# A hybrid decoder trunk on one core: TensorE's instructions kept in the program's order

## The chip, the core and the metric

The kernel runs on one core of a Trainium2 chip. The core has a matrix engine (TensorE, PE in the profile, with its weight loads shown apart as PEld), three engines for the rest (VectorE or DVE, ScalarE or ACT, GpSimd or POOL) and a queue that issues most of its transfers (SyncE or SP). Each engine works through a list of instructions of its own and waits on semaphores for the others. The metric is the device time of one launch in microseconds (us); less is better. Three runs of the kernel before gave a median of 1935.17 us, from 1935.16 to 1936.64.

## What is computed

Two layers work on 528 tokens (16 meta tokens and 512 of the sequence) of 1024 channels in float32:

```python
for layer in range(2):
    g = norm_gains[layer]
    h = h + 0.5 * rmsnorm(swiglu(rmsnorm(h, g[0]), w_ffn_in[layer, 0], w_ffn_out[layer, 0]), g[1])
    hn = rmsnorm(h, g[2])
    mix = gla_mixer(hn, ...) if layer == 0 else swa_mixer(hn, ..., k_sh, v_sh, ...)
    h = h + rmsnorm(mix, g[3])
    h = h + 0.5 * rmsnorm(swiglu(rmsnorm(h, g[4]), w_ffn_in[layer, 1], w_ffn_out[layer, 1]), g[5])
    if layer == 0:
        k_sh, v_sh = shared_kv(h, kv_norm, w_kv, cos, sin)
```

So there are four feed-forward blocks (FFNs) of 2816 hidden channels. The mixer of layer 0 is chunked gated linear attention with 4 heads; that of layer 1 is attention of 16 query heads in a window of 128 tokens, over keys and values made once. The output drops the meta tokens.

## The kernel before, in words

Channels lie on the 128 partitions and tokens along the free dimension, so a vector of 1024 channels is 8 tiles. Layer 0 works on two groups of tokens, 272 and 256 wide; layer 1 on two of 256, or on all 512 at once where that can be done. Each float32 operand is split into an upper and a lower part (`w` and its rest, made by ScalarE at L226 or L245 and VectorE at L227 or L246), and each product is three matmuls: upper by upper, lower by upper, upper by lower (`mm3s`). All matmuls are issued at L162 (`mm`), transposes at L174.

An FFN runs in four chunks of hidden tiles (`FF_CHUNKS`: 4, 6, 6 and 6 tiles). The first chunk is computed plainly, and `out_proj` then multiplies its hidden tiles by the output weights into banks named `y`. The other three use Strassen's scheme (class `Strassen`): for a hidden tile `head` makes one product, `body` four, `tail` two, each of 12 matmuls. They accumulate in the PSUM banks `a`, `c` and `d`, and between two products ScalarE or VectorE takes an interim value out of a bank. For tile after tile the order is body(current), head(next), tail(current); for the last tile of a chunk there is no next head, and its tail uses a bank of its own, `e`:

```python
def body(self, t):
    self.product(t.c, t, "s1", "t1", True)
    act.activation(t.v, t.c, AF.Copy)                    # L749
    self.product(t.a, t, "s2", "t2", False)
    act.activation(t.u2, t.a, AF.Copy)                   # L751
    self.product(self.d, t, "12", "21", False)
    act.activation(t.g1, self.d, AF.Silu)
    self.product(t.a, t, "s3", "t3", False)
    dve.tensor_tensor(t.v, t.a, t.v, op=ALU.add)         # L755
...
    self.product(c, t, "s4", "22", last)                 # in tail; c is the bank e for the last tile
```

In the profile `a<-zl0f_t,w_s` is the product s2 or s3 of layer 0 (`zl1f_t` of layer 1), `d<-zl0f,w` the product 12, `e<-zl0f,w_s` the product s4 of a last tile, and `a<-zl0f_t,w` the product 22. There are 4 x 3 = 12 ends of such chunks.

A norm needs the sum of squares over all channels: ScalarE squares (L399 and L402), GpSimd adds (L403), short matmuls `st_` with a vector of ones sum over the partitions, VectorE or GpSimd works out the inverse root and a diagonal matrix `dg` (L361 to L383), and a matmul `r_` spreads it over the partitions. In layer 1's attention `sc` are the scores, `ptm` and `pt` transposes of the probabilities, `o` their products with the values; ScalarE and VectorE copy scores out at L1116 and L1117, VectorE scales at L1135 and masks at L1156 and L1157.

Two things set the order of the work. The first is the program itself: pieces of work are Python generators, and `Flow` resumes them by a clock of its own. Every call of `mm` and `transpose` moves that clock on (columns / 2400 us for split operands, else columns / 600 but at least 0.12), `flow.pump()` resumes what is due, and a generator that yields 3.0 goes on 3 us later by that clock. So chains of small steps, such as a norm's, are woven between the matmuls of a large product in the order in which the program issues its instructions. The second is the scheduler of the framework, which runs when the `TileContext` closes: it goes through the program with its own estimates of durations, and gives each engine the list of its instructions in the order in which they become ready, earlier ones in the program first. Where the next matmul of the program isn't ready by these estimates, a later one that is ready goes ahead of it. Semaphores are placed after that.

`kernel` builds the inputs' layout, opens the `TileContext`, calls `trunk_kernel`, which issues everything, and launches.

## Time and profile before

| | |
|---|---|
| median of three runs | 1935.17 us |
| profiled execution | 1931.38 us |
| its span, first to last instruction | 1929.5 us |
| mean granted clock of TensorE | 0.996 |
| DVE busy | 1420.1 us |
| ACT busy | 1001.7 us |
| POOL busy | 215.1 us |
| bytes moved | 174.61 MB, 90 GB/s |

By stages of the span (PE busy us out of the stretch, then DVE and ACT busy us):

| stretch, us | what it is | PE | DVE | ACT |
|---|---|---|---|---|
| 0 to 45 | start, first FFN's first tiles | 36.84 of 45 | 30.88 | 24.81 |
| 45 to 370 | first FFN | 323.21 of 325 | 245.05 | 170.68 |
| 395 to 590 | linear attention | 192.06 of 195 | 117.28 | 77.74 |
| 690 to 1000 | second FFN | 307.27 of 310 | 233.30 | 165.59 |
| 1085 to 1385 | third FFN | 298.95 of 300 | 228.59 | 160.75 |
| 1428 to 1532 | windowed attention | 96.28 of 104 | 90.48 | 61.96 |
| 1600 to 1929.5 | fourth FFN and the end | 316.55 of 329.5 | 241.17 | 165.19 |

A row of the timeline gives the start and the duration in us, the engine, the line of the kernel, the operation, the tiles written and read (buffer numbers left out) with their shapes, the number of instructions merged into the row, and in brackets how long the engine stood idle before it and on whom it waited. A row of waits gives the total, how often, and the longest, in us. A row of the chain of work gives start, duration, engine, tile and line. The duration of a merged row of matmuls includes the run-out of the last one, so two such rows can overlap by some 0.15 us.

### The profile page before, as it was taken

Reading aid. Unit: us, or ns where it says so; the run is one execution under the profiler, and the core shown is the slowest. Engines: PE = TensorE matmul, PEld = TensorE weight load, DVE = VectorE, ACT = ScalarE, POOL = GpSimd, SP = SyncE. Lnnn points to the kernel's source line nnn. Section 1 sums busy time; section 2 is a strip of 40 time slices with the busy share of each in tenths; the row PEclk is TensorE's granted clock in tenths of the full one; section 3 lists DMA queues with packets and bytes.
Section 4 is the critical chain, followed back from the end, with each engine's and each line's share of the span. In section 5 each row is a group of like instructions: output and inputs, shape, how many; then the busy total and the mean of one; then the engine's idle time right before and its main releaser. Section 6 shows DMA issues by size and latency. Waiting matters only on the chain.

```text
span 1929.5 us, 37402 instructions
## 1 busy us (share of the span) xinstructions
PE 1888.9 (98%) x14522; PEld 1798.1 (93%) x14522; DVE 1420.1 (74%) x2868; ACT 1001.7 (52%) x2268; POOL 215.1 (11%) x417
## 2 busy tenths in 40 slices
PE   8999999999999999999999999999998999999997
PEld 7999999999999999999999898989976898989897
DVE  7885858676464788585887786868788779858584
ACT  5663636653245555353574453535645665636363
POOL 2000000321111400000033000000352140000002
PEclk9999999999999999999999999999999999999998
DMA  4332333322113123323351123233421212333331
GB/s 163 104 100 88 103 96 106 114 74 69 45 52 113 56 72 95 102 91 102 99 176 45 61 88 115 87 112 99 132 66 34 77 45 72 98 105 107 101 112 44
DMA packets 102144, 174.61 MB, mean 90 GB/s; under 512 B 11472, under 2 KB 24272, under 8 KB 101968
## 3 DMA queue, kind: packets, MB, share of 16 engines
q1 hardware_dynamic: 101680, 172.11, 28.2%
q8 instruction: 113, 1.85, 0.4%
q14 instruction: 63, 0.52, 0.1%
q10 hardware_dynamic: 288, 0.13, 0.0%
HBM read 170.10 MB, written 2.10 MB: 89 GB/s over the span
## 4 chain that ended last, share of the span: by engine, by line
PE 70%; DVE 19%; ACT 6%; issue 3%; POOL 1%; DMA 0%; SPq 0%; DVEq 0%; ACTq 0%; POOLq 0%
PE y L162 30%; PE x L162 16%; PE a L162 11%; DVE raw L251 5%; PE c L162 4%; DVE w_s L246 3%; DVE w L246 3%; ACT w_s L245 3%; PE d L162 2%; DVE w L227 2%; PE o L162 1%; ACT w L226 1%; PE po L162 1%; DVE hidl0f L775 1%; PE sc L162 0%
## 5 line engine op out<-in xcount | busy, mean ns | idle before, releaser
L246 DVE TENSOR_TENSOR w_s<-raw,w_s 128x512 fp32r<-128x512 f32 x288 | 194.0, 690 | 129.7 <-ACT w_s L245 127.6
L227 DVE TENSOR_TENSOR w<-raw,w 128x512 fp32r<-128x512 f32 x378 | 244.9, 673 | 31.1 <-ACT w L226 29.3
L162 PE MATMUL y<-hidl0f,w 128*128 128x256 f32 (+1 forms) x2112 | 261.0, 285 | 0.0
L162 PEld LDWEIGHTS y<-hidl0f,w 128*128 128x128 f32 x2112 | 258.8, 188 | 0.7
L245 ACT ACTIVATE w_s<-raw 128x512 fp32r<-128x512 f32 x288 | 175.3, 628 | 149.5 <-DVE raw L251 146.0
L162 PE MATMUL y<-hidl1f,w 128*128 128x512 f32 (+1 forms) x1344 | 249.8, 346 | 0.0
L162 PEld LDWEIGHTS y<-hidl1f,w 128*128 128x128 f32 x1344 | 212.0, 188 | 33.9 <-ACT hidl1f L774 0.4
L226 ACT ACTIVATE w<-raw 128x512 fp32r<-128x512 f32 x378 | 209.0, 586 | 46.0 <-PE y L162 39.4
L403 POOL TENSOR_TENSOR acc_post<-acc_post,sq_post 128x256 f32<-128x256 f32 (+1 forms) x72 | 56.9, 791 | 1386.5 <-ACT sq_post L402 1386.0
L251 DVE TENSOR_TENSOR raw<-raw,raw 128x512 f32<-128x512 f32 x288 | 198.0, 687 | 5.5
L246 DVE TENSOR_TENSOR w<-raw,w 128x512 fp32r<-128x512 f32 x216 | 148.3, 687 | 41.5 <-ACT w L245 40.2
L245 ACT ACTIVATE w<-raw 128x512 fp32r<-128x512 f32 x216 | 133.9, 621 | 48.0 <-PE y L162 47.7
L162 PE MATMUL x<-x_l0m,w 128*128 128x272 f32 (+1 forms) x1200 | 158.3, 288 | 0.0
L162 PEld LDWEIGHTS x<-x_l0m,w 128*128 128x128 f32 x1200 | 149.4, 189 | 1.2
L572 DVE TENSOR_TENSOR Y<-y,Y 128x256 f32<-128x256 f32 (+2 forms) x176 | 83.0, 473 | 74.4 <-PE y L162 73.8
L162 PE MATMUL a<-zl0f_t,w_s 128*128 128x264 f32 x864 | 117.8, 285 | 3.8 <-ACT c L751 3.8
L162 PE MATMUL a<-zl1f_t,w_s 128*128 128x256 f32 x864 | 115.1, 282 | 2.0 <-ACT c L751 1.6
L162 PEld LDWEIGHTS a<-zl0f_t,w_s 128*128 128x128 f32 x864 | 110.1, 188 | 5.0 <-ACT c L751 5.0
L162 PEld LDWEIGHTS a<-zl1f_t,w_s 128*128 128x128 f32 x864 | 106.9, 188 | 4.8 <-ACT c L751 4.8
L162 PE MATMUL x<-x_l0f,w 128*128 128x256 f32 (+1 forms) x768 | 100.0, 290 | 7.5 <-ACT w L226 5.8
L162 PEld LDWEIGHTS x<-x_l0f,w 128*128 128x128 f32 x768 | 96.6, 191 | 8.9 <-ACT w L226 5.8
L162 PE MATMUL x<-x_l1f,w 128*128 128x256 f32 (+1 forms) x576 | 93.1, 320 | 0.0
(485 smaller groups left out, 3306.5 us busy)
## 6 DMA issues: line engine op xcount, KB each, us to landing
raw<-in_w_in SPq DMA_DIRECT2D x352, 256.0 KB, 2.9
raw<-in_w_out SPq DMA_DIRECT2D x96, 256.0 KB, 3.3
raw<-in_gla_in SPq DMA_DIRECT2D x50, 256.0 KB, 3.0
raw<-in_w_last SPq DMA_DIRECT2D x48, 256.0 KB, 3.1
raw<-in_w_out SPq DMA_DIRECT2D x64, 128.0 KB, 3.0
raw<-in_gla_out SPq DMA_DIRECT2D x16, 256.0 KB, 2.9
raw<-in_w_q SPq DMA_DIRECT2D x16, 256.0 KB, 3.6
raw<-in_swa_out SPq DMA_DIRECT2D x16, 256.0 KB, 2.8
```

Source lines behind the costliest of these rows:

```text
L162: inst = pe.matmul(o, lhs, rhs, start=start, stop=stop, skip_group_check=onto)
L226: act.activation(w[:, 0, :m], raw[:, :m], AF.Copy)
L227: dve.tensor_tensor(w[:, 1, :m], raw[:, :m], w[:, 0, :m].bitcast(F32), op=ALU.subtract)
L245: act.activation(w[:, 0, :512], src, AF.Copy)
L246: dve.tensor_tensor(w[:, 1, :512], src, w[:, 0, :512].bitcast(F32), op=ALU.subtract)
L251: dve.tensor_tensor(dst, dst, src, op=ALU.add)
L403: pool.tensor_tensor(sums[0][:, :n], sums[0][:, :n], t[:, :n], op=ALU.add)
L572: dve.tensor_tensor(y, p[:, :n], y, op=ALU.add)
L775: dve.scalar_tensor_tensor(t.hid[:, 1, g], t.h, -1.0, t.hid[:, 0, g].bitcast(F32), op0=ALU.mult, op1=ALU.subtract)
```

## The change

The call of `trunk_kernel` is put inside a block that takes TensorE out of the scheduler's arranging: PE's list is the order in which the program issues its matmuls and transposes. The lists of the other engines are arranged as before, by the same rule, and so are the transfers. No instruction is added, removed or changed, and no size or buffer.

```diff
     with tile.TileContext(nc) as tc:
-        trunk_kernel(tc, aps, out)
+        with tc.manual_schedule(engines={mybir.EngineType.PE}):
+            trunk_kernel(tc, aps, out)
     r = run_bass_kernel_spmd(nc, [{f"in_{n}": v for n, v in arrays.items()}], core_ids=[0])
```

## The prediction

> **What bounds the kernel now.** I read the page's busy line and its chain first, then the waits of TensorE, then the timeline at those waits.
>
> ```profile
> PE 1888.9 (98%) x14522; PEld 1798.1 (93%) x14522; DVE 1420.1 (74%) x2868; ACT 1001.7 (52%) x2268; POOL 215.1 (11%) x417
> ...
> PE 70%; DVE 19%; ACT 6%; issue 3%; POOL 1%; DMA 0%; SPq 0%; DVEq 0%; ACTq 0%; POOLq 0%
> ```
>
> TensorE (PE) stands idle for 1929.5 - 1888.9 = 40.6 us in all. Nearly everything else is hidden behind it, so a microsecond in which PE newly waits is a microsecond on the end, and at most 40 us could ever be won. Of the waits of PE, listed by their total, two lines matter here (total us, times, longest):
>
> ```profile
> PE x L162 <- ACT w L226: 5.8, 1, 5.8
> PE a L162 <- ACT c L751: 5.4, 12, 0.7
> ```
>
> The first is the start of the kernel, which no order of matmuls can help. The second is twelve waits of the same kind, and the change acts on them.
>
> **What the change moves.** Nothing is added or removed: the same 14522 matmuls run. I wrote out the order in which the program issues them, by following its own clock (`Flow`) through the code, and laid it beside the order of the matmuls in the trace. 13749 stand at the same place. Where they differ, the scheduler had done nearly always the same: where a matmul would have had to wait, it ran later matmuls first. The change takes those fillers out and puts them behind the wait. So at each place the loss is the smaller of two times: what the fillers take, and how long the waiting matmul still has to wait when PE reaches it. If PE in the trace still stands idle after the fillers, the loss is the whole of the fillers.
>
> **(1) The twelve ends of Strassen chunks.** `body` issues the products s1, s2, 12 and s3, and the last `tail` then issues s4 into a bank of its own, `e`. s3 adds onto bank `a`, and so it waits until ScalarE has copied that bank out (L751). In the timeline of the first such end (start, duration, engine):
>
> ```profile
> 140.74 1.64 PE L162 MATMUL d<-zl0f,w 128*128 128x264 f32 x12
> ...
> 142.21 0.76 PE L162 MATMUL e<-zl0f,w_s 128*128 128x264 f32 x5
> 142.31 0.37 ACT L749 ACTIVATE c<-c 128x264 f32<-128x264 f32 x1
> 142.58 0.62 ACT L226 ACTIVATE w<-raw 128x512 fp32r<-128x512 f32 x1
> 143.10 0.38 ACT L751 ACTIVATE c<-a 128x264 f32<-128x264 f32 x1
> ...
> 143.53 1.71 PE L162 MATMUL a<-zl0f_t,w_s 128*128 128x264 f32 x12 [0.56 <-ACT c L751]
> ```
>
> The reader is to see that five matmuls of `e` run ahead of s3 (`a`), that PE still idles 0.56 us after them, and that s3 starts 0.05 us after L751 ends at 143.48. L751 does not depend on the five, so s3 starts at 143.53 either way and the five come after it. The same holds at all twelve ends: s3 starts 0.04 to 0.06 us after L751 ends. The fillers counted in the timeline are 5, 5 and 9 in each FFN of layer 0, and 8, 8 and 12 in each of layer 1. Durations come from the chain of work, undisturbed stretches of the same products:
>
> ```profile
> 731.51 2.92 PE a L162 x24
> ...
> 1135.41 2.85 PE a L162 x24
> ```
>
> That is 0.1217 and 0.1187 us each. Layer 0: 2 x 19 x 0.1217 = 4.6 us. Layer 1: 2 x 28 x 0.1187 = 6.6 us. Together **11.3 us**. Queued behind s3 are e, the product 22 and the whole out-projection; VectorE waits for them, and ends none of it earlier. At eight of the ends 2 to 10 matmuls of `y` were also run ahead of 22, which waits for VectorE's sum at L755. That costs nothing: in program order all of e (1.4 us) stands between s3 and 22, and L755 ended 0.65 us after s3 in the first end. Without that cover it would be 4 x 10 x 0.12 = 5 us or less.
>
> **(2) The first out-projection of two FFNs.** `y` needs the last hidden tile, and the trace puts six matmuls that read it behind matmuls that don't:
>
> ```profile
> 61.44 5.78 PE L162 MATMUL y<-hidl0f,w 128*128 128x272 f32 x46
> ...
> 63.57 0.43 ACT L407 ACTIVATE hidl0f<-gu 128x272 fp32r<-128x272 f32 x1 [3.30 <-DVE gu L622]
> ...
> 64.35 0.43 DVE L408 TENSOR_TENSOR hidl0f<-gu,hidl0f 128x272 fp32r<-128x272 f32 x1
> ```
>
> In program order PE reaches the tenth matmul at 62.57 and waits until 64.06 for the upper part, runs two, and waits from 64.31 until 64.84 for the lower: 1.5 + 0.5 = 2.0 us. In the FFN at 692 us the same rows stand at 692.73 and 693.50 against 692.78, which gives 0.45 + 0.5 = 0.95. Four more ends of chunks lose one matmul each, 0.5. Together **3.4 us**. A further place, at 1585 us, where three 512-wide matmuls of 0.23 us ran ahead of one waiting for VectorE (L426, until 1585.86): 0.6 us.
>
> **(3) Norms and one transpose.** The sums `st_` and the factors `r_` are short matmuls that wait for ScalarE, VectorE or GpSimd. One of five:
>
> ```profile
> 1035.86 1.42 PE L162 MATMUL x<-x_kv,w 128*128 128x256 f32 x10
> 1037.12 0.79 PE L162 MATMUL st_kv<-ones,acc_kv 128*128 128x1 f32 x6
> ...
> 1036.62 0.40 ACT L399 ACTIVATE acc_kv<-H 128x256 f32<-128x256 f32 x1
> ```
>
> Its operand is there at 1037.02, so in program order PE waits from 1035.86 to 1037.07: 1.2 us, and the ten follow. The others: ten x before `r_l0f` at 39.88 (its `dg` ends at 39.82), 1.2; seven before `pk` at 435.33, which even then waited 1.25, 0.85; seven before `st_l0f` at 664.67, 0.85; eleven before `st_l1m` at 1419.85 (operand at 1419.56), 1.15. Together **5.25 us**.
>
> **(4) Attention, 1428 to 1480 us.** Here the orders differ most, but the same x matmuls move to other waits. Seven 512-wide ones stood before the first transpose of the probabilities:
>
> ```profile
> 1446.82 2.58 PE L162 MATMUL x<-x_l1m,w 128*128 128x512 f32 x10
> ...
> 1450.05 0.33 PE L174 MATMUL ptm<-ident,mt 128*128 128x128 f32 x1 [0.65 <-DVE mt L1135]
> ```
>
> They take 7 x 0.233 = 1.6 us and all of it is lost there. One of them then covers 0.2 of the 2.06 us that the scores wait at 1454.58, and three stand where PE idled 0.35 to 0.7 between scores and `o`. Two breaks of x or `o` by other shapes also go, each of which costs 0.36 + 0.17 to 0.36 us of idle weight loading. VectorE is busy for 10.00 of 10.00 us from 1480 to 1490, where PE idles 2.75 us, so part of a late arrival is taken up there. I take **+0.5 us**, with bounds of -3 and +6: everything saved, or scores of the fourth head, behind `o` in program order, 3.6 us late with all their VectorE work behind them.
>
> **The sum** is 11.3 + 3.4 + 0.6 + 5.25 + 0.5 = 21 us on the profiled execution's 1931.38, or 1952.4. That execution was 3.8 us under the median of the three runs, 1935.17, so against the runs I forecast **1956.2 us**, 1.1% slower.
>
> [...] At the wait quoted in (1) the weight load and the matmul of s3 both start at 143.53. [...] Second, the granted clock was 0.64 from 1456 to 1460, after 1452 to 1456 in which PE was busy for 1.91 of 4.00 us. [...] By the rows a further such stretch, possible before 1450, costs 4 x 0.36 + 4 x 0.06 = 1.7 us; I put it in the upper end only.
>
> **Rivals.** (A) The scheduler arranges the other engines by the times that it expects; with PE held back these move, and ScalarE's copies may come out earlier. If half of (1) and (2) goes, 7 to 11 us are saved: about 1947. For it: L751 stood behind a weight split (L226, 0.62 us) that nobody needed yet. Against: that queue is filled before the wait, by work that doesn't depend on the fillers. (B) Attention turns into a chain, scores late and each later softmax with them, and the clock drops once more: +6 to +10 over the forecast, about 1964. For it: PE idles 7.7 us of 104 there already, and VectorE is busy for 90. (C) Faster: ScalarE's order moves so far that L751 comes straight after s2 everywhere. It could have started at 140.8 instead of 143.10. Then (1) is nothing, the 5.4 us of present waits (9.9 counted at the weight loads) go too, and if (2) also goes and attention saves its 3, the sum is 0.6 + 5.25 - 9.9 - 3 = -7: about 1928. It decides from where L751 ends before the last matmul of 12, that is 1.3 us earlier than now. Nothing in the change asks for it. (D) The order does not change, or only in places that don't wait: 1935.
>
> **Chances.** Forecast 0.57, A 0.16, B 0.13, C 0.07, D 0.07. A measurement of this kernel tells about 0.2%, 3.9 us, from no change. Faster by more is C, 0.07; within it are D and the low end of A, 0.10; slower 0.83. The range reaches from A's lower half to B: 1942 to 1967.
>
> **What would show it.** In the changed profile PE's busy time stays near 1889 and its idle time grows from 41 to about 62 us; the line of waits of `a` on L751 grows from 5.4 to about 16 us with still 12 or more waits; `e` runs as twelve in one piece after s3; `st_kv` and its like wait 1 to 2 us each. If the span of the stretch 690 to 1000 us grows by less than 3 us, term (1) is wrong. What would make the whole wrong is a changed order on ScalarE: L751 no longer behind L226.

## The result and the profile after

The median of four runs of the changed kernel is 1956.06 us (1955.20 to 1956.68), that of four runs of the kernel before beside them 1935.74 us (1935.16 to 1936.64). The ratio is 1.0104, with an interval from 1.0087 to 1.0122: slower by 20.3 us, where 21 were forecast. The profiled execution took 1955.57 us with a span of 1953.7.

The page of the kernel after, its busy line and its chain:

```profile
PE 1893.7 (97%) x14522; PEld 1802.5 (92%) x14522; DVE 1420.8 (73%) x2868; ACT 1002.2 (51%) x2268; POOL 214.9 (11%) x417
...
PE 71%; DVE 20%; ACT 6%; issue 3%; POOL 0%; DMA 0%; SPq 0%; DVEq 0%; ACTq 0%
```

The work is the same: as many matmuls, the same busy time of VectorE, ScalarE and GpSimd. TensorE (PE) stands idle for 1953.7 - 1893.7 = 60.0 us, where it was 40.6. The waits of PE in the kernel after (total, times, longest):

```profile
PE a L162 <- ACT c L751: 16.9, 12, 1.8
...
PE ptm L174 <- DVE mt L1135: 4.8, 2, 3.1
...
PE pk L174 <- DVE f L880: 2.1, 1, 2.1
PE st_l0f L162 <- ACT acc_l0f L399: 2.0, 1, 2.0
```

and the same two groups in the kernel before:

```profile
PE pk L174 <- DVE f L880: 1.3, 1, 1.3
...
PE st_l0f L162 <- ACT acc_l0f L399: 1.1, 1, 1.1
```

The twelve waits of `a` on L751 grew from 5.4 to 16.9 us in all, those of `pk` and `st_l0f`, a transpose and a norm's sum, by 0.85 and 0.9; `st_kv` and `st_l1m`, which waited for ScalarE nowhere before, stand there with 1.1 and 1.0. The timeline of the kernel after at the first end of a Strassen chunk:

```profile
144.33 0.65 ACT L774 ACTIVATE hidl0f<-c 128x528 fp32r<-128x528 f32 x1 [0.76 <-DVE c L771]
...
145.15 0.62 ACT L226 ACTIVATE w<-raw 128x512 fp32r<-128x512 f32 x1
...
145.67 0.38 ACT L751 ACTIVATE c<-a 128x264 f32<-128x264 f32 x1
...
146.10 1.74 PE L162 MATMUL a<-zl0f_t,w_s 128*128 128x264 f32 x12 [1.26 <-ACT c L751]
...
147.68 1.62 PE L162 MATMUL e<-zl0f,w_s 128*128 128x264 f32 x12
```

`e` runs in one piece of 12 behind s3, and s3 starts 0.05 us after L751 ends, as it did before. ScalarE's order here is what it was: L751 still comes behind L774, L749 and the weight split of L226. In the whole program, told apart by line and tile names, at least 34 of ScalarE's 2270 instructions and 56 of VectorE's 2868 have to be moved to turn the one list into the other, most of them in the attention and in the first out-projections; of GpSimd's and SP's none. At eight of the chunk ends two steps of VectorE change places (the sum L764 and the weight split L227), both behind s3. So at the chunk ends what changed ahead of s3 is PE's own order, not an order elsewhere.

### The profile page after: what moved, and what is told of

It reads as the page before. It is cut to its first block, busy times and chain, and to the rows that moved or that the text cites. A ratio compares the mean times of both kernels' runs of the same rounds, so it can differ in the third digit from the quotient of the medians.

```text
span 1953.7 us, 37401 instructions
## 1 busy us (share of the span) xinstructions
PE 1893.7 (97%) x14522; PEld 1802.5 (92%) x14522; DVE 1420.8 (73%) x2868; ACT 1002.2 (51%) x2268; POOL 214.9 (11%) x417
## 4 chain that ended last, share of the span: by engine, by line
PE 71%; DVE 20%; ACT 6%; issue 3%; POOL 0%; DMA 0%; SPq 0%; DVEq 0%; ACTq 0%
PE y L162 30%; PE x L162 16%; PE a L162 11%; DVE raw L251 4%; PE c L162 4%; DVE w_s L246 3%; DVE w L246 3%; ACT w_s L245 3%; PE d L162 3%; DVE w L227 2%; PE o L162 1%; PE e L162 1%; PE po L162 1%; ACT w L226 1%; DVE hidl0f L775 1%
## 5 line engine op out<-in xcount | busy, mean ns | idle before, releaser
L227 DVE TENSOR_TENSOR w<-raw,w 128x512 fp32r<-128x512 f32 x378 | 244.0, 671 | 34.3 <-ACT w L226 32.4
L226 ACT ACTIVATE w<-raw 128x512 fp32r<-128x512 f32 x378 | 209.2, 586 | 51.3 <-PE y L162 41.8
```

The lines of the kernel that those rows point to most:

```text
L226: act.activation(w[:, 0, :m], raw[:, :m], AF.Copy)
L227: dve.tensor_tensor(w[:, 1, :m], raw[:, :m], w[:, 0, :m].bitcast(F32), op=ALU.subtract)
```

## The experiments

The theory of the prediction is that the time is lost where a later matmul no longer fills a wait, most of it at the ends of the Strassen chunks. Against it stand the rivals of the prediction, and one more that the traces after suggested: that the longer idle times cost by the clock that they bring, not by themselves. The kernel before gave a median of 1935.31 us (21 runs, 1930.50 to 1936.95) beside the first four experiments and 1935.41 (9 runs, 1932.40 to 1936.58) beside the others; the ratios are to these.

### Which part of the program loses

`e1_ffn_pinned` keeps the program's order of matmuls in the four FFNs alone, `e2_mixers_pinned` in the linear attention, the shared keys and values and the windowed attention alone.

```diff
+    def pinned():
+        return tc.manual_schedule(engines={mybir.EngineType.PE})
 # e1, at each of the four calls
-    ffn(x, L0, fin, True)
+    with pinned():
+        ffn(x, L0, fin, True)
 # e2, at the other three
-    gla(x, fin)
+    with pinned():
+        gla(x, fin)
```

> TensorE keeps the program's order only while the four FFNs are issued; elsewhere the scheduler arranges it. Theory 1 (the loss is what the fillers took, place by place): 11.3 of the chunk ends, 3.4 of the first out-projections, 0.6 at 1585 us, 1.2 and 0.85 of the two norms at the start of FFNs, together 17.4 us over the kernel before. Theory 2 (a good part of the loss is TensorE's clock, which is halved for 3.4 us after a stretch with a long wait, at 344, 443 and 675 us of the changed kernel): the stretches at 344 and 675 stay, and 1.2 us each come on top, some 20 us over.

> The complement: order kept only while the two mixers and the shared keys and values are issued. Theory 1: 0.85 of the transpose at 435 us, 1.2 and 1.15 of two norms, 0.5 of the attention, 3.7 us over the kernel before. The changed kernel's trace speaks for less, since from 1419 to 1485 us it gains 1.9 us on the kernel before: about 1.3. Theory 2: 1.2 more for the stretch at 443 us. If the two parts do not add up to the 20.3 us of the whole, the rest is in how the parts act on each other.

Measured: e1 1955.59 us (1955.37 to 1960.91), ratio 1.0109, interval 1.0096 to 1.0123. e2 1936.03 us (1932.48 to 1938.19), ratio 1.0003, interval 0.9994 to 1.0011. The twelve waits of `a` on the copy are 16.9 us in e1, as in the change, and 5.3 in e2, as before it.

All of the 20.3 us lies in the FFNs (20.3 in e1), within the measurement; the mixers with their norms give 0.7, no change that can be told. e1 is 2.9 us over the 17.4 of theory 1 and near the 20 of theory 2. That does not make the clock the cause: the second execution of the kernel after, shown further down, has its half-clock pieces at 440, 672, 1051, 1440 and 1474 us, none close behind a chunk end, and yet the twelve ends lose 13.8 us in it against the second execution of the kernel before, as much as in the first pair. What theory 1 lacks in the FFNs is told in the section on why the prediction was right: 2.1 us more at the chunk ends and 1.9 in two out-projections that it does not name, less 0.9 at 62 us.

### Giving the fillers back by program order

If the program itself issues the first matmuls of `e` ahead of s3, the pinned order has the fillers back at the chunk ends. `e3_lead` leads with as many as the scheduler had run there (5, 5, 9 in layer 0; 8, 8, 12 in layer 1), `e6_lead4` with 4 at every end.

```diff
-    def body(self, t):
+    def body(self, t, lead=0):
...
         act.activation(t.g1, self.d, AF.Silu)
+        if lead:
+            dve.tensor_tensor(t.u2, t.c, t.u2, op=ALU.add)
+            t.e = ps(f"e{t.name}")[:, : self.n]
+            self.product(t.e, t, "s4", "22", True, 0, lead)    # matmuls 0 to lead - 1
         self.product(t.a, t, "s3", "t3", False)
...
-            self.product(c, t, "s4", "22", last)
+            self.product(c, t, "s4", "22", last, t.lead)       # the rest
```

> The changed kernel, with the program itself issuing the first 5, 5 and 9 (layer 0) or 8, 8 and 12 (layer 1) matmuls of the last tile's product e ahead of s3, as the scheduler did. Theory 1: the wait of s3 is filled again and 11.3 us come back, the rest of the loss stays: about 1945. Theory 2: the stretch of half clock at 344 us goes too, 1.2 us more. If the waits at the chunk ends had nothing to do with the loss, the time stays at 1956.

> The changed kernel with only the first 4 matmuls of e ahead of s3 at all twelve ends, instead of 5 to 12 in the run e3, which gave back 3.5 us by its median where 11.3 were expected and showed 3.5 us of new waits of the product 22 on VectorE's sum. Theory 1a (a filler gives back its own time as long as enough of e is left between s3 and 22, some 0.65 us or 6 matmuls): 12 x 4 x 0.12 = 5.8 us come back, more than with the longer leads: about 1950, and no wait of 22 on VectorE. Theory 1b (each filler gives back its time whatever follows): 5.8 of 11.3, so less than e3 should have given, and e3's shortfall comes from elsewhere. If moving e ahead loses as much as it fills, 1956.

Measured: e3 1952.56 us (1949.73 to 1952.74), ratio 1.0084, interval 1.0070 to 1.0097; e6 1952.37 us (1950.16 to 1953.25), ratio 1.0088, interval 1.0074 to 1.0102. Against 1956.06 that is 3.5 and 3.7 us won: a miss for e3, which was to win the whole 11.3, and less than expected for e6 (5.8). The waits of PE in e3 show where the gain went (L751 is L752 there, and L755 is L761):

```profile
PE a L162 <- ACT c L752: 5.3, 12, 0.7
...
PE a L162 <- DVE c L761: 3.5, 4, 1.4
```

The wait of s3 is back at 5.3, as before the change. But product 22, which also writes `a`, now waits for VectorE's sum. The timeline of e3 at the third end of the first FFN, behind s3:

```profile
343.50 0.54 PE L162 MATMUL e<-zl0f,w_s 128*128 128x264 f32 x3
344.32 1.74 PE L162 MATMUL a<-zl0f_t,w 128*128 128x264 f32 x12 [0.28 <-DVE c L761]
345.89 2.45 PE L162 MATMUL y<-hidl0f,w 128*128 128x272 f32 x17
348.57 5.68 PE L162 MATMUL y<-hidl0f,w 128*128 128x272 f32 x43 [0.23 <-DVE hidl0f L778]
```

What is led is missing behind s3: only three of `e` stand there as cover for VectorE's sum, and `y` then meets the last hidden tile before it is made. Counted at the weight loads, the waits on L752 fall from 20.9 to 8.9 us, those on L761 rise from nothing to 5.3 and those of `y` on layer 0's last hidden tile from 0.7 to 1.9: 12.0 won, 6.5 given back, 5.5 left. Measured from the same matmuls ahead of each of the twelve ends to the same ones behind it, the trace of e3 is 4.7 us shorter than the kernel after in its second execution, which has no half-clock piece there; the medians of four runs each are 3.5 apart. e6, with a shorter lead, wins as much: its waits of `a` on L752 are 11.0 us, there are none of note on L761, and by the same matmuls the twelve ends are 4.1 us shorter.

### The wait by its cause

The wait exists because ScalarE reaches L751 late: it first does L774, the copy of the hidden tile before, which waits for VectorE. `e4_hid_later` is the change with L774 held behind L751 of the next tile, and `e5_before_hid_later` is the same move in the kernel before, whose matmuls the scheduler arranges.

```diff
-        act.activation(t.u2, t.a, AF.Copy)                    # L751
+        u2 = act.activation(t.u2, t.a, AF.Copy)
+        if self.gate is not None:
+            self.gate.u2 = u2
+            self.gate.finish(flow)
+        t.gate = self.gate = Job(None)
...
+            if not last:
+                yield t.gate                                  # goes on once the next u2 is issued
...
-            act.activation(t.hid[:, 0, g], t.h, AF.Copy, scale=-1.0)   # L774
+            hid = act.activation(t.hid[:, 0, g], t.h, AF.Copy, scale=-1.0)
+            if not last:
+                after(t.gate.u2, hid)                         # order only
```

> The changed kernel, with ScalarE's copy of a finished hidden tile (L774) put behind the next tile's copy of bank a (L751), so that L751 no longer stands behind an instruction that waits for VectorE. TensorE's order is as in the changed kernel. Theory 1 says that s3's wait is set by ScalarE's queue alone: L751 then ends before the product 12 does, the 16.9 us of waits of a on L751 go to about 0, and the time falls by about 17 us to 1939, whatever TensorE's order is. If L751 is late because of the weight splits (L226) in front of it, half of that stays: about 1948.

> The kernel before (all engines arranged by the scheduler) with the same move on ScalarE as in the run e4: the copy of a finished hidden tile (L774) behind the next tile's copy of bank a (L751). Theory 1: the twelve waits of a on L751, 5.4 us in the kernel before, go, and nothing else changes: about 1930, and then the order of TensorE at the chunk ends is worth nothing, so what is left between this and the run e4 (1938.4) is the first out-projections, the norms and the transpose, 3.4 + 0.6 + 5.25 = 9 us. If the scheduler's fillers were worth something of their own, beyond filling this wait, the distance would be over 15 us.

Measured: e4 1938.39 us (1935.29 to 1941.86), ratio 1.0019, interval 1.0010 to 1.0029. e5 1925.36 us (1923.39 to 1928.17), ratio 0.9950, interval 0.9938 to 0.9963: **faster than both kernels**, by 0.5% of the kernel before. e4 is where theory 1 had it (1939). e5 is not: theory 1 had 1930, and 9 us between e4 and e5, where 13.0 were measured. Among the waits of PE no line of `a` on the copy (L752 here) is left, in e4 nor in e5; the longest in both is now that of the kernel's start. The first chunk end in the timeline of e5:

```profile
139.96 1.63 PE L162 MATMUL d<-zl0f,w 128*128 128x264 f32 x12
...
140.38 0.38 ACT L752 ACTIVATE c<-a 128x264 f32<-128x264 f32 x1
...
140.65 0.64 ACT L781 ACTIVATE hidl0f<-c 128x528 fp32r<-128x528 f32 x1
...
141.43 1.64 PE L162 MATMUL a<-zl0f_t,w_s 128*128 128x264 f32 x12
```

The copy runs while product 12 is still being worked, ahead of the hidden tile's (L781), and s3 follows product 12 without a wait and without a filler. So in the pinned order the wait on L751 is worth 1956.06 - 1938.39 = 17.7 us (16.9 in the line of waits), and in the scheduler's order 1935.41 - 1925.36 = 10.0 us. The waits of `a` as PE's weight loads have them (PEld), before and after:

```profile
PEld a L162 <- ACT c L751: 9.9, 20, 0.9
```

```profile
PEld a L162 <- ACT c L751: 20.9, 18, 2.0
```

In the scheduler's order the 10.0 won are near the 9.9 of the weight loads and far from the 5.4 of the matmuls; in the pinned order the 17.7 won are near the 16.9 of the matmuls and under the 20.9 of the weight loads. So neither count is a price by itself. At the twelve ends, by the same matmuls ahead and behind, e5's trace is 7.8 us shorter than that of the kernel before; the other 2 us are not placed. Pinning costs 1938.39 - 1925.36 = 13.0 us even where s3 never waits.

### Idle time or clock

The trace after has pieces at half clock close behind chunk ends. `e7_dummy` issues nine matmuls on zeros into a spare bank ahead of s3 at all twelve ends; the output does not change. They keep PE busy where it would wait.

```diff
...
+        for _ in range(idle):                                 # 9 at the last tile of a chunk
+            pe.matmul(spare, zeros, zz, start=True, stop=True)
         self.product(t.a, t, "s3", "t3", False)
```

> The changed kernel with 9 matmuls on zeros, into a bank that nothing reads, issued ahead of s3 at each of the twelve chunk ends. The output does not change. They take 1.1 us, less than the 1.3 to 1.8 us that s3 waits there. Theory 1 (the wait is ScalarE's alone): s3 starts no later, PE's busy time grows by up to 13 us and the time stays at 1956. Theory 2 (the idle time costs more through the clock): the stretches of half clock that follow a chunk end (343.5 us in the changed kernel's trace) go, about 1.2 us each, so up to 2 us under. If busy matmuls take something from the other engines, the time is longer.

Measured: 1956.72 us (1953.76 to 1958.98), ratio 1.0112, interval 1.0096 to 1.0127. From its page:

```profile
PE 1907.9 (98%) x14630; PEld 1816.7 (93%) x14630; DVE 1419.2 (73%) x2868; ACT 1002.3 (51%) x2268; POOL 216.2 (11%) x417
```

PE is busy 14.2 us longer, the waits of `a` on L751 are 3.3 us instead of 16.9, and the time is the same: what is lost at the ends is the place in the order and nothing that filling it with idle work would bring back. In this trace no half-clock piece follows a chunk end of the first FFN, as one does after, but others do elsewhere, and in all they are five.

### The first out-projection

`e8_defer` is the change, with the program itself putting the matmuls of the last hidden tile in the first out-projection of layer 0's FFNs behind those of the first three units.

```diff
+        early = {}
+        if first and not finish and len(groups) == 2:
+            for m, g in ((0, groups[0]), (0, groups[1]), (1, groups[0])):
+                early[m, g] = ps(f"y{used[0]}_{m}_{g[0]}")
+                part(early[m, g], m, g, 0, nh - 1)            # all tiles but the last
...
-                unit(m, g)
+                unit(m, g, early.get((m, g)))                 # the last tile, then the rest
```

> The changed kernel with the first out-projection of an FFN of layer 0 issued in another order by the program: the last hidden tile's matmuls of the first three units come after the other tiles' of all three, as the scheduler had put six of them. Theory 1: the two waits there, 2.0 and 0.95 us, go: about 1953. If these waits were not there, 1956. Twelve or nine more matmuls stand ahead than the scheduler had put, which costs nothing by this theory.

Measured: 1958.84 us (1957.43 to 1963.62), ratio 1.0127, interval 1.0113 to 1.0142: a miss, 2.8 us over the change. At the place itself it does what it was made for. The timeline of the kernel after, and then of e8:

```profile
64.50 0.52 PE L162 MATMUL y<-hidl0f,w 128*128 128x272 f32 x2 [0.27 <-ACT hidl0f L407]
65.29 1.92 PE L162 MATMUL y<-hidl0f,w 128*128 128x272 f32 x14 [0.27 <-DVE hidl0f L408]
```

```profile
63.77 5.40 PE L162 MATMUL y<-hidl0f,w 128*128 128x272 f32 x43
```

The two waits are gone, and by the same matmuls the two places are 0.87 and 0.98 us shorter. But this execution has seven pieces at half clock, where the profiled one of the change has four. That three pieces more take away more than 1.9 us is what the next section makes likely; why this kernel meets more of them stays open, and its other three runs have no trace.

### One kernel, several executions

The kernel before was run twice more and the kernel after once more, unchanged, for the number of half-clock pieces in each execution.

> The kernel before, once more, for its profile. The profiled execution of before that the prediction used took 1931.38 us, 4 us under the median, and its trace has one stretch of 3.4 us at half clock between the start and the last norm; the changed kernel's has four. Theory 2 (each such stretch costs some 1.5 us, and which waits are followed by one depends on where they fall in a fixed grid of 3.41 us, which the launch does not reset): another execution of the same kernel shows the same waits, but another number of stretches at other places, and its time follows: some 1930 + 1.5 for each. Theory 1 alone (times follow the waits only): the same time within the scatter, whatever the number of stretches.

> The same as e9, a third execution of the kernel before: by theory 2, 1930 + 1.5 us for each stretch at half clock, at places that need not be those of the others.

> The changed kernel once more. Theory 2: its waits as in the first trace (16.9 us of a on L751), a number of half-clock stretches that may differ from four, and a time of some 1949.5 + 1.5 us for each.

Measured, one execution each: 1934.77, 1936.03 and 1959.33 us. The twelve waits of `a` are 5.3 us in the second and third execution of the kernel before and 16.9 in the second of the kernel after, where the first ones had 5.4 and 16.9. So the order's part repeats, and what differs between executions is elsewhere. Beside the last stretch (0.50 from 1917.9 us to the end in the first execution of the kernel before, from 1944.6 us in that of the kernel after), the record of the granted clock holds short pieces at 0.5. Windows of the kernel after around two of them (stretch, length, then busy us of PE, PEld, DVE, ACT and POOL with their instructions, granted clock, DMA share, GB/s):

```profile
336.90:340.30 3.40, 3.40 (x30) 3.40 (x29) 3.40 (x7) 2.48 (x6) 0.00 (x0) 1.00 0.68 165
340.30:343.70 3.40, 1.60 (x13) 1.38 (x13) 3.20 (x7) 2.59 (x7) 0.00 (x0) 1.00 0.86 272
343.70:347.10 3.40, 3.40 (x18) 3.40 (x17) 2.63 (x6) 2.43 (x6) 0.00 (x0) 0.50 0.88 254
439.30:442.70 3.40, 1.31 (x12) 1.06 (x10) 3.40 (x9) 1.36 (x3) 0.00 (x0) 1.00 0.49 154
442.70:446.10 3.40, 3.40 (x18) 3.40 (x17) 2.00 (x5) 3.17 (x7) 0.00 (x0) 0.50 0.32 89
```

In both places a stretch of 3.4 us in which PE is busy for less than half is followed by one at half clock, in which 18 matmuls run instead of 30. That is no rule, though. The third chunk end in the second execution of the kernel after, by windows of the same grid:

```profile
340.92:344.33 3.41, 1.61 (x13) 1.61 (x14) 3.21 (x6) 3.38 (x8) 0.00 (x0) 1.00 0.87 291
344.33:347.74 3.41, 3.41 (x31) 3.41 (x30) 3.19 (x7) 1.64 (x4) 0.00 (x0) 1.00 0.88 281
```

Here PE is as little busy, and the clock stays. The same matmuls with and without such a piece, at this chunk end, from the timeline of the kernel after in its first and its second execution:

```profile
343.31 2.72 PE L162 MATMUL a<-zl0f_t,w_s 128*128 128x264 f32 x12 [1.80 <-ACT c L751]
...
347.87 1.63 PE L162 MATMUL a<-zl0f_t,w 128*128 128x264 f32 x12
```

```profile
342.72 1.74 PE L162 MATMUL a<-zl0f_t,w_s 128*128 128x264 f32 x12 [1.80 <-ACT c L751]
...
345.75 1.63 PE L162 MATMUL a<-zl0f_t,w 128*128 128x264 f32 x12
```

From s3 to product 22 it is 4.56 us with the piece and 3.03 without: it costs 1.53 us, after the same wait of 1.80. With the pieces counted in each trace (two in a row count as two), and 1.5 us taken off for each, the profiled times come together:

| profiled execution | time, us | pieces | time less 1.5 each |
|---|---|---|---|
| before, first execution | 1931.38 | 1 | 1929.9 |
| before, second execution | 1934.77 | 4 | 1928.8 |
| before, third execution | 1936.03 | 5 | 1928.5 |
| e2, mixers pinned | 1936.08 | 5 | 1928.6 |
| after, first execution | 1955.57 | 4 | 1949.6 |
| after, second execution | 1959.33 | 7 | 1948.8 |
| e1, FFNs pinned | 1960.91 | 8 | 1948.9 |
| e3, lead | 1949.73 | 3 | 1945.2 |
| e6, lead of 4 | 1952.68 | 5 | 1945.2 |
| e7, dummies | 1956.12 | 5 | 1948.6 |
| e8, deferred tile | 1957.70 | 7 | 1947.2 |
| e4, pinned, copy first | 1937.30 | 4 | 1931.3 |
| e5, copy first | 1925.36 | 4 | 1919.4 |

Three executions of the kernel before that lie 4.7 us apart agree within 1.4, and the two of the kernel after within 0.8. The difference of the two kernels is then 1949.2 - 1929.1 = 20.1 us. What is left falls with the number of pieces, so 1.5, which comes from one place in dense matmuls, is too much on the average: the differences within a kernel are 3.39 us for three pieces, 4.65 for four and 3.76 for three, 1.1 to 1.3 each. At 1.2 each both kernels agree within 0.3, and their difference is 20.8. In the last column e8 is 2.0 under the kernel after, about the 1.9 of its two places.

## Why the prediction was right, and where it was not

The forecast of 1956.2 met the median of 1956.06. That it came within 0.2 us is luck: two terms were too low, two too high, and one was missing. Its terms, each against the growth at its places between the first two traces, by the same matmuls before and after, a half-clock piece taken out at 1.5 us where one lies in it:

| term | forecast, us | measured, us |
|---|---|---|
| (1) chunk ends, layer 0 | 4.6 | 5.2 |
| (1) chunk ends, layer 1 | 6.6 | 8.7 |
| (2) first out-projections, layer 0 | 2.0 + 0.95 | 1.05 + 0.97 |
| first out-projections, layer 1 | no term | 1.2 + 0.7 |
| (2) ends of chunks, one matmul each | 0.5 | in (1) |
| (2) at 1585 us | 0.6 | 0.4 |
| (3) `r_l0f`, `pk`, `st_l0f` | 1.2, 0.85, 0.85 | 1.2, 0.85, 0.9 |
| (3) `st_l1m`, `st_kv` | 1.15, 1.2 | 1.15, 1.1 |
| (4) attention | +0.5 | -1.9 |
| sum | 21 | 21.5 |

The two traces differ by 24.2 us, or by 19.7 without the three pieces that lie in these places (the fourth of the kernel after stands against the one of the kernel before). Of the 1.8 us by which the sum is more, waits that shrink close behind a loss give some 0.6: that of `r_kv` behind `st_kv` 0.4, that of `r_l0f` behind `st_l0f` 0.2. The rest is not placed.

**(1) The mechanism is right and its size too small.** The forecast's own test, the growth of the stretch with the second FFN by 3 us, is met: its three chunk ends and its first out-projection give 0.60 + 0.38 + 1.42 + 0.97 = 3.4. The waits on L751 alone grew by 16.9 - 5.4 = 11.5, the forecast of 11.3. What failed is the step that the matmuls of `y` ahead of product 22 cost nothing. It asked whether 22 would wait, and rightly said no. It did not ask who waits behind 22: `y` itself, for the last hidden tile that 22 leads to. The timeline of the kernel before and of the kernel after at the third end of the third FFN:

```profile
1356.71 1.35 PE L162 MATMUL y<-hidl1f,w 128*128 128x256 f32 x10
...
1359.31 3.94 PE L162 MATMUL y<-hidl1f,w 128*128 128x256 f32 x32
```

```profile
1378.39 2.29 PE L162 MATMUL y<-hidl1f,w 128*128 128x256 f32 x17
1380.91 3.79 PE L162 MATMUL y<-hidl1f,w 128*128 128x256 f32 x30 [0.23 <-DVE hidl1f L775]
```

Before, ten of `y` were done early and the rest ran through; after, the seventeen that don't need the tile end 0.23 us too soon (0.4 counted at the weight load). Counted at the weight loads, the waits of `y` on L774 and L775 grew from 0.8 to 3.3 us; the ends came out 13.9 - 11.3 - 0.5 = 2.1 us over the forecast, of which these waits are the part that the traces name. e3 shows the same from the other side: with s3's fillers back, the next two consumers took more than half of it.

**(2)** was too high by 0.9, all of it at 62 us. The upper part (L407) came 63.57 - 61.44 = 2.13 us after the first `y` before the change, and 64.02 - 62.95 = 1.07 after it: PE had lost 1.2 at `r_l0f` just ahead, and the other engines had not lost as much. The forecast added terms that follow each other closely as if each were alone; a loss ahead comes off the next wait. It also took no loss for the same place in the two FFNs of layer 1, without a reason. The first of them, in the kernel before and in the kernel after:

```profile
1087.35 4.91 PE L162 MATMUL y<-hidl1f,w 128*128 128x512 f32 x20
```

```profile
1102.24 2.26 PE L162 MATMUL y<-hidl1f,w 128*128 128x512 f32 x9
1105.28 3.07 PE L162 MATMUL y<-hidl1f,w 128*128 128x512 f32 x11 [0.78 <-ACT hidl1f L407]
```

Twenty ran through where after nine PE now waits for the upper part; with a shorter wait for the lower part the place grew by 1.2 us, and the one at 1609 us by 0.7. The second executions show the same. **(3)** was right in each part: the wait is the filler's time where PE idled already (`pk` from 1.25 to 2.1), and as long as the operand takes where it didn't (`st_kv`).

**(4)** had the wrong sign, within its bounds. The timeline of the kernel after at the first transpose of the probabilities, whose rows of before are in the forecast:

```profile
1472.87 0.33 PE L174 MATMUL ptm<-ident,mt 128*128 128x128 f32 x1 [3.15 <-DVE mt L1135]
```

The wait ahead of the transpose grew from 0.65 to 3.15, more than the 1.6 of the seven fillers. But the scores behind it wait less, before and after:

```profile
PE sc L162 <- DVE pt L1157: 2.5, 1, 2.5
PE sc L162 <- DVE Y L1117: 2.2, 2, 2.1
```

```profile
PE sc L162 <- DVE pt L1157: 1.4, 1, 1.4
...
PE sc L162 <- DVE Y L1117: 0.8, 1, 0.8
```

From the sums `st_l1m` at 1396.87 before and 1417.64 after to the `x` on zeros that opens the last FFN (1558.62 and 1578.69) it is 161.75 and 161.05 us, with one half-clock piece in each; less the 1.15 of `st_l1m` that is -1.9. The forecast let the seven `x` fill 0.2 us of later gaps; its lower bound, everything saved, was nearer. The waits named do not make up the whole of it (+4.1 for `ptm`, -2.5 for the scores), no run takes the attention apart, and some of the 34 and 56 moved instructions lie in it, so where it comes from is open. e2, which pins it with the other mixers and norms, is 0.7 us over the kernel before, where the terms of these places make +3.1 and -1.9.

**The clock** was handled right for the wrong reason. The forecast took the profiled execution's 1931.38 and put the 3.8 us to the median on top. The later executions show what these are: that one met one half-clock piece, two others of the same kernel met four and five. The profiled execution after met four, so the two first traces differ by 24.2 us and the medians by 20.3. Had the spans been compared with each other, 4 us of clock would have been taken for a cost of the order. A further piece was priced at 1.7 us and costs 1.5 at the one place that could be compared.

**The rivals.** (A) and (C) needed ScalarE's order to move at the chunk ends; it didn't, as the row of L751 behind L226 shows. (C) named the right place and near enough the price for it: with the copy moved by hand the kernel before wins 10.0, where (C) counted 9.9 at the weight loads. (B), a chain in the attention, is refuted by e2. (D) is refuted by the waits.

In e4 and e5, which differ by the pinning alone and have no wait of s3, 13.0 us are lost to it. Of these (2) to (4) explain 5.7, and the waits of `y` on the last hidden tile another 4, which at the weight loads are 5.1 us in e4 and under 1 in e5. The first out-projections of layer 1 add 1.9. Some 1.5 us are not placed; the two profiled executions, with four half-clock pieces each, are 11.9 apart and leave next to nothing.

## What to carry to other kernels

Before you price a filler that leaves a wait, follow the chain to the end: the matmuls that were taken from behind the wait also covered the next consumer, and the one after it. A filler that a scheduler finds is a sign of a wait with a cause; here the cause was one copy in ScalarE's list, queued behind an instruction that waited for VectorE (0.76 us at the first chunk end), and moving that copy won 10.0 us where none of the orders of matmuls tried here won anything. Compare two traces only after counting the pieces at half clock in each (here 1.1 to 1.5 us a piece).

## What the hardware showed

In the record of the granted clock each short piece at half clock in the first executions of the two kernels is 3.413 us long, and the pieces of the kernel after lie on a grid of that step. They begin at 343.7, 442.7, 674.8 and 1473.5 us: 99.0, 232.1 and 798.7 us apart, which are 29, 68 and 234 steps of 3.413. Counted from the first instruction the grid lies elsewhere in another execution: a window of it begins at 340.3 us here and at 340.92 in the second execution of the same kernel, whose pieces at 440, 672, 1051, 1440 and 1474 us are 29, 97, 208, 322 and 332 steps behind that.

In the windows ahead of these four pieces PE was busy for 1.60, 1.31, 1.43 and 0.63 of 3.40 us. The other windows of that grid from 10 to 1941 us have 1.69 (1896.77 to 1900.18) or more, and no piece follows them. Yet in the first execution of the kernel before the one piece, at 1457.09, stands behind a window with 1.94 us busy, and a window with 1.77 (1480.98 to 1484.40) is followed by none. At the third chunk end, after the same wait of 1.80 us, a window with 1.60 busy was followed by one and a window with 1.61 was not. In the second execution of the kernel after the seven pieces stand at five places: from 1440 us on, six `st_l1m` and 36 `x` take 1.25 and 8.52 us, where the same ones took 0.83 and 5.85 in the first execution, 3.1 us more, about what two pieces in a row would cost. So the busy time of one window does not decide it alone, and what decides is not shown.

So one kernel has four pieces in one execution and seven in the next. In the kernel before they were one, four and five, and its three times are 4.7 us apart; its runs without a trace scatter by 6.5 us (1930.50 to 1936.95).
